# High parts of output-projection inputs on VectorE inside attention, two first sums on ScalarE, and the turns of the rotary tables two products behind their copies

## The chip, the cores and the metric

The kernel runs on one core of one Trainium2 chip. Times are device microseconds (us) of one execution of the whole program; of several runs the median is given. A core has TensorE (PE, matrix products), VectorE (DVE), ScalarE (ACT), GpSimd (POOL) and SyncE (SP, which here only starts DMAs). Matrix products land in PSUM; everything else works out of SBUF. Each engine takes its own instructions strictly in the order in which the program lists them, and waits on semaphores for the others.

## The reference

One decoder block, 2048 positions, 1024 channels, f32 throughout. The input projection makes eight column groups; one group goes through a short convolution and a gated linear recurrence, three through attention in three dilated windows with partial rotary positions, the rest are gates.

```python
proj = h @ w_in[l]
x_rnn, z_rnn, q, k, v, z_attn, g_r, g_a = jnp.split(proj, IN_SPLITS, axis=-1)
hr = rg_lru(causal_depthwise_conv(x_rnn, ...), w_a, b_a, w_x, b_x, lam, positions)
y_rnn = (hr * jax.nn.silu(z_rnn)) @ w_out_rnn[l]
qh, kh = apply_partial_rope(q, cos, sin), apply_partial_rope(k, cos, sin)
o = dilated_attention_mixture(qh, kh, vh).reshape(B, S, D_ATTN)
y_attn = (o * jax.nn.silu(z_attn)) @ w_out_attn[l]
merged = jax.nn.sigmoid(g_r + bg_r) * y_rnn + jax.nn.sigmoid(g_a + bg_a) * y_attn
x = x + gate[:, None, :] * (merged @ w_o[l])
return rms_norm(x, g_final)
```

Rotary positions need `cos` and `sin` of position times frequency. The change touches how a table of these is brought into the layout of q and k, how sums of products are taken out of PSUM in the input projection, and how the inputs of `y_rnn` and `y_attn` are made ready for TensorE.

## The kernel before

**Split operands.** TensorE multiplies in a rounded f32 format (`fp32r`). To keep f32 accuracy each operand is split into a high part, a copy that rounds (`hi_act` on ScalarE, L162, or `hi_dve` on VectorE, L165), and a low part, the rest that the subtraction leaves (`lo_pool` on GpSimd, L168, or `lo_dve` on VectorE, L171). A product is three matmuls, high by high, high by low, low by high (`mm3`, all at L154). These helpers stand behind nearly every row of a view: rows are told apart by their tiles, not by their lines.

**Input projection.** It runs in two halves of the positions, `f` = 0 and 1, as Strassen-like pairs of column blocks: `strassen` makes seven products for each pair, each of 12 matmuls, into the PSUM tiles X, Z, W, V, Y. The order on TensorE is X (`B11`), the V (`B22`) that the pair before has left over, Z, W, V (`T1`), X (`B21`), Y. Four sums are needed; the first is a copy of X to SBUF, `u1`, to which Z is added for `u2`. The left operands S are made from raw loads R by GpSimd, VectorE and ScalarE in the first half, stored to DRAM (`sD`) by DMAs on ScalarE's queue, and in the second half reloaded from there for the first 20 pairs. All side work is hung on the count of products: `after_prod[n]` and `late[n]` hold functions that are called after product n, and the scheduler of the framework then keeps each engine's order near to that.

**Recurrence and tables.** Between the pairs the recurrence of each block of channels runs on VectorE and ScalarE. The rotary tables are made in each half, four pieces each (two column halves q, and i = 0 for cosine, 1 for sine), which begin at products 90, 94, 111 and 116 behind the half's start (`PIECES`). A piece has three steps: `repeat` (L1087, VectorE copies a 128x64 block of the table, repeated four times, into a 128x512 tile), `turn` (L1092, four 128x128 transposes on TensorE into the PSUM tile `pg`), and `store` (L1098, ScalarE copies `pg` to SBUF for the cosine; L1100, VectorE multiplies it by a sign for the sine; then L1101, a DMA on SP's queue to the table `tabD`). In the first half the tiles of `repeat` and `store` come from a ring of three buffers `ev`, from which the gates' tiles (L460, stored to `zaT` at L1255) are taken as well; in the second half they are raw tiles R, the ring of five into which weights are loaded as well.

**Attention with the output projection inside.** From about 1345 to 1880 us the 16 head-halves (8 heads, two halves of the queries) run as a sequence of slots under `manual_schedule`, which keeps the program order exactly. Each slot has five places: HEAD, the scores of one tile and their softmax (L1489 on VectorE, L1490 on ScalarE), SOFTMAX, EXCHANGE, WEIGHTS, then the transposes of the probabilities of the tile seven slots earlier (`pT` at L1575 and L1588, split into `pth` and `ptl`) and the products with the values (`sc`, `o`), TAIL. Between these places `spend` fills TensorE with steps of the output projection: job j is one block of 512 positions of `yaT` (j = 0 to 3, the recurrence's branch) or `oT` (j = 4 to 7, the attention's), with 8 output tiles m of 8 steps k, three matmuls each, into the PSUM tile `pj`. Jobs 0 to 3 and most of job 4 run inside attention, job 5 to 7 behind it.

**Inputs of a job.** A job's input is eight 128x512 tiles (k = 0 to 7). `load_y` loads one into a buffer R0 to R3; `split_y` splits it into `yh` and `yl` (rings of nine). Two tables of step numbers, relative to the job's start, say when each load and each split is listed:

```python
    LOAD_Y = {-12: [0], -10: [1], -8: [2], -6: [3], -2: [4], 4: [5], 5: [6], 6: [7]}
    SPLIT_Y = {-3: [0], 3: [1], 4: [2], 5: [3], 7: [4], 10: [5], 11: [6], 12: [7]}
```

So a split's high and low part stand in the engines' order wherever the step lands between the places of a slot. GpSimd makes the low part of even k and VectorE that of odd k; GpSimd splits the heads' `kq`, `vh` and `wh` beside it.

Of the kernel before, what the change touches and what calls it, by code (L numbers as in the profile page):

```python
# [14 lines left out]
AF = mybir.ActivationFunctionType  # L15
# [9 lines left out]
NB = 4  # L25
# [10 lines left out]
MORE = 0.8  # L36
FIRST = 4.0
REBUILT = 20
COPIED = (5, 22)
NEG = 1e30  # L40

TABLES = 24
# [50 lines left out]
def decoder_block(ctx, tc, x, c, positions, g_norm, w_mod, b_mod, w_in, b_gate, conv_w, conv_b,  # L93
                  w_a, b_a, w_x, b_x, lam, w_out_rnn, w_out_attn, w_o, g_final, cst, out):
    nc = tc.nc
# [65 lines left out]
    def hi_act(o, i):  # L161
        nc.scalar.activation(o, i, AF.Copy)  # L162
# [152 lines left out]
    def load_next():  # L315
        n = n_loaded[0]
        n_loaded[0] += 1
        if n < REBUILT * 7:
            t = s_tile([P, 2, KH, P])
            nc.sync.dma_start(t[:].bitcast(F32), sD[n])  # L320
            loaded.append((n, t))
        elif n >= 28 * 7:
            k = n - 28 * 7
            for y in range(2 * k - 2, 2 * k) if k in (1, 2) else ():
                load_yd(yaT, 0, y)
            if k < 3:
                load_wd(0, 0, k) if k < 2 else load_wd(0, 1, 0)
            if k == 1:

                t = T(hp, [P, KH, CH], F32, "T", bufs=14)  # L330
                nc.sync.dma_start(t[:], yaT[KH * P :, :CH].rearrange("(k p) j -> p k j", p=P))
                for i in range(KH):
                    Y0[True, 0, KH + i] = t[:, i, :]
# [17 lines left out]
    def strassen(f, key, done):  # L351

        up = pu[0]
        x = pair_id[key]
        if f and x == 0:
            for _ in range(NS):
                load_next()
        n_op = iter(range(7 * x, 7 * x + 7))

        def take():  # L360
            if f and x < REBUILT:
                return (f, *loaded.pop(0))
            i = next(n_op)
            return f, i, first.pop(i)

        def prod(ps, b, first, last, op=None):
            f, i, s = op or take()
            bh, bl = B[b]
            for k in range(KH):
                mm3(ps[:], s[:, 0, k, :], s[:, 1, k, :], bh[:, k, :], bl[:, k, :],  # L370
                    first=first and k == 0, last=last and k == KH - 1, skip_group_check=True)
            n_prod[0] += 1
            if f:
                used.add(i)
                while n_loaded[0] - NS in used:
                    load_next()
            run_late(n_prod[0])

        X = T(pj, [P, CH], F32, "X", bufs=2)
        prod(X, "B11", True, False)  # L380
        last_product()
        Z = T(pj, [P, CH], F32, "Z")
        prod(Z, "T2", True, True)
        u1 = T(up, [P, CH], F32, "u1", bufs=1)
        u2 = T(up, [P, CH], F32, "u2", bufs=2)
        with tc.high_priority():
            if not f and x in COPIED:
                nc.vector.tensor_copy(u1[:], X[:])
            else:
                nc.scalar.activation(u1[:], X[:], AF.Copy)  # L390
            nc.vector.tensor_tensor(u2[:], Z[:], u1[:], ALU.add)
        W = T(pj, [P, CH], F32, "W")
        prod(W, "T3", True, True)
        u3 = T(up, [P, CH], F32, "u3", bufs=1)
        with tc.high_priority():
            nc.vector.tensor_tensor(u3[:], W[:], u2[:], ALU.add)
        V = T(pj, [P, CH], F32, "V")
        prod(V, "T1", True, False)
        done(1, 1, V, u3)
        prod(X, "B21", False, True)  # L400
        done(0, 0, X, None)
        Y = T(pj, [P, CH], F32, "Y")
        prod(Y, "T4", True, True)
        done(1, 0, Y, u3)
        op = take()

        def last():
            prod(V, "B22", False, True, op)
            done(0, 1, V, u2)
        behind.append(last)  # L410
# [4 lines left out]
    def last_product():  # L415
        while behind:
            behind.pop()()
# [622 lines left out]
    def rotary_tables(rp, f):  # L1040

        v = {}

        def angles():
            pi = T(rp, [P, 2, 4], I32, "pi")
            nc.sync.dma_start(pi[:], positions[0].rearrange("(n j r) -> j n r", n=NB, r=4)[:, 2 * f : 2 * f + 2, :])
            v["pi"] = pi
            for tag in ("an", "kk", "co"):
                v[tag] = T(rp, [P, 8, 16], F32, tag)

        def convert():
            v["pf"] = T(rp, [P, 8], F32, "pf")
            nc.vector.tensor_copy(v["pf"][:], v["pi"][:].rearrange("p n r -> p (n r)"))

        def products():
            nc.vector.tensor_tensor(
                v["an"][:], v["pf"][:].unsqueeze(2).broadcast_to([P, 8, 16]),
                cs[:, K_IF : K_IF + 128].rearrange("p (b f) -> p b f", f=16), ALU.mult)

        flat = lambda tag: v[tag][:].rearrange("p b f -> p (b f)")  # L1060
        magic = 1.5 * 2.0 ** 23
        tensor = lambda dst, src, s1, s2, *ops: lambda: nc.vector.tensor_scalar(flat(dst), flat(src), s1, s2, *ops)

        def reduce(per, bits, n):
            yield tensor("kk", "an", float(1 / per), None, ALU.mult)
            yield tensor("kk", "kk", magic, None, ALU.add)
            yield tensor("kk", "kk", -magic, None, ALU.add)
            for cc in split_const(per, bits, n):
                yield lambda cc=cc: nc.vector.scalar_tensor_tensor(flat("an"), flat("kk"), -cc, flat("an"), ALU.mult, ALU.add)

        def shifted():
            nc.vector.scalar_tensor_tensor(flat("co"), flat("an"), math.pi / 2, flat("kk"), ALU.add, ALU.add)

        lim = 3.1415925
        quarter = (tensor("kk", "an", math.pi / 2, -float(TWO_PI), ALU.is_gt, ALU.mult), shifted,
                   *(tensor(tag, tag, lim, -lim, ALU.min, ALU.max) for tag in ("an", "co")))

        def sines():
            for tag in ("an", "co"):
                nc.scalar.activation(flat(tag), flat(tag), AF.Sin)  # L1080

        def piece(q, i):

            def repeat():
                src = v[("co", "an")[i]]
                v["rep"] = raw_tile([P, 4, 8, 16]) if f else T(rp, [P, 4, 8, 16], F32, "ev", bufs=3)
                nc.vector.tensor_copy(v["rep"][:], src[:, 4 * q : 4 * q + 4, :].unsqueeze(2).broadcast_to([P, 4, 8, 16]))  # L1087

            def turn():
                v["pt"] = T(pg, [P, 4, P], F32, "pg")  # L1090
                for r in range(4):
                    nc.tensor.transpose(v["pt"][:, r, :], v["rep"][:, r].rearrange("p a b -> p (a b)"), ident)  # L1092

            def store():
                t = raw_tile([P, CH]) if f else T(rp, [P, CH], F32, "ev", bufs=3)
                pt = v["pt"][:].rearrange("p r j -> p (r j)")
                if i == 0:
                    nc.scalar.activation(t[:], pt, AF.Copy)  # L1098
                else:
                    nc.vector.tensor_scalar(t[:], pt, cs[:, K_SG : K_SG + 1], None, ALU.mult)  # L1100
                nc.sync.dma_start(tabD[f, i, :, q * CH : (q + 1) * CH], t[:])  # L1101

            return repeat, turn, store

        at_, base = TABLES, n_prod[0]
        for fn in (angles, None, convert, products, *reduce(TWO_PI * 4096, 7, 8), *reduce(TWO_PI, 11, 5), *quarter, None, sines):
            if fn:
                after_prod.setdefault(base + at_, []).append(fn)
            at_ += 1
        assert at_ <= PIECES[0]  # L1110

        for x, (q, i) in enumerate((q, i) for q in range(2) for i in range(2)):
            for d, fn in zip((0, 3, 4), piece(q, i)):
                after_prod.setdefault(base + PIECES[x] + d, []).append(fn)

    def load_tables(qp, f):
# [59 lines left out]
    for t in range(6):  # L1176
        pieces = []
        i0 = t * P
        while i0 < (t + 1) * P:
            hd, i = divmod(i0, 96)  # L1180
# [547 lines left out]
    def steps(jobs):  # L1728
# [39 lines left out]
        def split_y(j, k):  # L1768
            if j < len(jobs):
                Y[j, k] = yh, yl = [T(fl, [P, CH], F32R, tag, bufs=NY) for tag in ("yh", "yl")]  # L1770
                w, ys, n = jobs[j]
                t = Y0.pop((ys is yaT, n, k))
                hi_act(yh[:], t[:])
                (lo_dve if (k % 2 if j else k > 4) or j > NB + 1 else lo_pool)(yl[:], t[:], yh[:])

        def load_g(t):
# [27 lines left out]
        for t, (j, m) in enumerate(tiles):  # L1804
            ps = T(pj, [P, CH], F32, "pj")
            for k in range(KT):
                x = 2 * t + k // KH
# [25 lines left out]
                yh, yl = Y[j, k]  # L1833
# [5 lines left out]
                x = m * KT + k - KT * (KT - 1)  # L1839
                j1 = j + 1  # L1840
                if m == 0:
                    x, j1 = x + KT * KT, j
# [309 lines left out]
    with tc.manual_schedule():  # L2152
# [10 lines left out]
        for p in range(NP):  # L2163
            for d, fn, args in left_events(p):
                x = 7 * p + d - 4
# [54 lines left out]
```

## Time and profile before

| | us |
|---|---|
| median of three runs | 2177.58 |
| the three runs | 2177.54, 2182.49, 2177.58 |
| the profiled execution, as timed | 2177.2 |
| its span, first to last instruction | 2175.4 |
| granted clock of TensorE, mean | 0.999 |
| DMA, mean over the span | 240 GB/s |

The profile is of one further execution. Its page gives the busy time of each engine and the chain of waits that ends last. A view of waits gives, for each engine, what an instruction waited for: engine, tile, line, then the sum in us, the number of waits and the longest. In a timeline a row is start, length, engine, line, operation, written tile, then "<-" and the tiles read, and in square brackets the idle time of the engine before it with whoever ended it. `sc`, `pT`, `pj`, `pg`, X, Y, Z, W and V are PSUM tiles; the others lie in SBUF or, for `zaT`, `yaT`, `tabD`, `sD`, in DRAM. A row of one tile's instructions gives least, median and greatest duration in ns, and the first and last start.

### The profile page before, as it was taken

How to read it: one execution, taken by the hardware profiler on the slowest of the kernel's cores; microseconds unless marked ns; L12 is line 12 of the kernel's file. 1: busy time of each engine (PE TensorE's matmuls, PEld its weight loads, DVE VectorE, ACT ScalarE, POOL GpSimd, SP SyncE). 2: the span in 40 equal slices, each digit the busy share in tenths (PEclk: the TensorE clock that was granted, in tenths of full speed). 3: DMA queues.
4: the chain of work that ended last, by engine and by line, in shares of the span. 5: the costliest groups of instructions: out<-in, count | busy, mean ns of one | idle time of the engine just before them, and what ended most of it. 6: DMA issues, size and time to landing. Idle time of an engine off the chain costs nothing.

```text
span 2175.4 us, 32659 instructions
## 1 busy us (share of the span) xinstructions
PE 2144.5 (99%) x10570; PEld 1788.8 (82%) x10571; DVE 1482.4 (68%) x2570; ACT 1311.0 (60%) x2621; POOL 1110.7 (51%) x868
## 2 busy tenths in 40 slices
PE   9999999999999999999999999999999999999998
PEld 6888788788788888888888887888888988888886
DVE  6769877768656715545546675577767777688887
ACT  5748678568644527457457532688888887444333
POOL 1467677667666323223223575466666674422444
PEclk9999999999999999999999999999999999999999
DMA  8467887787655368898996566988886777898552
GB/s 302 142 213 262 275 300 268 270 285 244 176 116 164 107 230 289 297 307 307 321 327 238 160 165 182 286 270 265 264 269 213 254 235 231 301 320 296 181 172 109
DMA packets 413040, 522.98 MB, mean 240 GB/s; under 512 B 103142, under 2 KB 278466, under 8 KB 411844
## 3 DMA queue, kind: packets, MB, share of 16 engines
q1 hardware_dynamic: 372852, 403.22, 59.2%
q10 hardware_dynamic: 34384, 99.78, 12.3%
q0 software_dynamic: 5632, 17.88, 2.4%
q8 instruction: 84, 1.38, 0.3%
q14 instruction: 88, 0.72, 0.1%
HBM read 332.02 MB, written 188.75 MB: 239 GB/s over the span
## 4 chain that ended last, share of the span: by engine, by line
PE 57%; DMA 4%; DVE 4%; ACT 3%; issue 3%; POOL 2%; SPq 0%; POOLq 0%; ACTq 0%; DVEq 0%
PE X L154 11%; PE V L154 11%; PE pj L154 8%; PE Z L154 6%; PE W L154 6%; PE Y L154 5%; PE sc L154 3%; PE o L154 3%; DMA fg<-gaT 1%; PE pg L154 1%; DMA fg<-mrT 1%; ACT pp L1490 1%; PE pT L1575 1%; DMA vraw<-vN 1%; PE pT L1588 1%
## 5 line engine op out<-in xcount | busy, mean ns | idle before, releaser
L168 POOL TENSOR_TENSOR S<-R,S 128x512 fp32r<-128x512 f32 x192 | 296.0, 1549 | 176.8 <-ACT S L162 85.5
L154 PE MATMUL X<-T,S 128*128 128x512 f32 x1344 | 324.2, 390 | 3.4 <-ACT u L390 1.6
L154 PE MATMUL V<-T,S 128*128 128x512 f32 x1344 | 324.8, 390 | 0.5 <-DVE ev L460 0.2
L154 PE MATMUL pj<-yh,S 128*128 128x512 f32 x896 | 324.2, 403 | 0.0
L154 PEld LDWEIGHTS X<-T,S 128*128 128x128 f32 x1344 | 251.4, 188 | 58.8 <-ACT u L390 3.6
L154 PEld LDWEIGHTS V<-T,S 128*128 128x128 f32 x1344 | 251.4, 188 | 55.6 <-DVE xr L460 1.1
L168 POOL TENSOR_TENSOR S<-s,S 128x512 fp32r<-128x512 f32 x116 | 170.6, 1471 | 149.3 <-ACT S L162 106.4
L154 PEld LDWEIGHTS pj<-yh,S 128*128 128x128 f32 x896 | 168.2, 188 | 30.1 <-DVE S L171 1.1
L154 PE MATMUL pj<-yl,S 128*128 128x512 f32 x448 | 175.8, 392 | 0.4 <-POOL yl L168 0.2
L162 ACT ACTIVATE S<-s 128x512 fp32r<-128x512 f32 x124 | 77.4, 624 | 150.6 <-DVE s L287 104.9
L1490 ACT ACTIVATE pp<-pp,st 128x256 f32<-128x256 f32 (+3 forms) x256 | 133.5, 523 | 54.8 <-DVE st L1489 53.9
L154 PE MATMUL W<-T,S 128*128 128x512 f32 x672 | 162.1, 390 | 0.0
L154 PE MATMUL Y<-T,S 128*128 128x512 f32 x672 | 161.5, 389 | 0.0
L154 PE MATMUL Z<-T,S 128*128 128x512 f32 x672 | 161.4, 389 | 0.0
L162 ACT ACTIVATE S<-R 128x512 fp32r<-128x512 f32 x200 | 121.5, 623 | 59.4 <-issue 15.2
L171 DVE TENSOR_TENSOR ptl<-pT,pth 128x384 fp32r<-128x384 f32 (+1 forms) x160 | 97.9, 629 | 81.7 <-ACT pth L162 79.5
L154 PEld LDWEIGHTS W<-T,S 128*128 128x128 f32 x672 | 125.7, 188 | 26.8 <-issue 0.9
L154 PEld LDWEIGHTS Z<-T,S 128*128 128x128 f32 x672 | 126.1, 188 | 26.2
L154 PEld LDWEIGHTS Y<-T,S 128*128 128x128 f32 x672 | 126.1, 188 | 26.1
L168 POOL TENSOR_TENSOR s<-R,s 128x512 fp32r<-128x512 f32 x32 | 44.3, 1386 | 186.4 <-ACT s L162 166.6
L979 DVE SCALAR_TENSOR_TENSOR xc<-xr,par,xc 128x512 f32<-128x512 f32 x96 | 103.2, 1075 | 53.2 <-ACT xc L973 50.9
L1555 ACT ACTIVATE pp<-pp,M 128x256 f32<-128x256 f32 (+3 forms) x256 | 118.1, 523 | 7.5 <-DVE M L1678 7.3
(424 smaller groups left out, 4939.6 us busy)
## 6 DMA issues: line engine op xcount, KB each, us to landing
sD<-S ACTq DMA_DIRECT2D x140, 512.0 KB, 3.6
S<-sD SPq DMA_DIRECT2D x140, 512.0 KB, 5.2
S<-wD SPq DMA_DIRECT2D x82, 512.0 KB, 5.4
R<-in_w_in_dram SPq DMA_DIRECT2D x144, 256.0 KB, 3.3
wD<-s ACTq DMA_DIRECT2D x64, 256.0 KB, 4.7
kraw<-kqT SPq DMA_DIRECT2D x32, 384.0 KB, 5.1
T<-in_w_mod_dram SPq DMA_DIRECT2D x16, 512.0 KB, 8.9
vN<-ev SPq DMA_DIRECT2D x32, 256.0 KB, 2.6
```

What stands on the lines that cost most here:

```text
L154: nc.tensor.matmul(o, lhsT=l, rhs=r, start=st, stop=sp, **kw)
L162: nc.scalar.activation(o, i, AF.Copy)
L168: nc.gpsimd.tensor_tensor(o, i, h.bitcast(F32), ALU.subtract)
L171: return nc.vector.tensor_tensor(o, i, h.bitcast(F32), ALU.subtract).ins
L979: nc.vector.scalar_tensor_tensor(xc, xr[:, i : i + CH], cw(i), xc, ALU.mult, ALU.add)
L1490: nc.scalar.activation(pdst, pdst, AF.Exp, bias=m_, scale=-1.0, accum_out=l_)
L1555: nc.scalar.activation(pp, pp, AF.Copy, scale=w)
L1575: nc.tensor.transpose(pt[:, c0 + j * P : c0 + (j + 1) * P], pp[i][:, k * P : (k + 1) * P], ident)
L1588: nc.tensor.transpose(pt[:, c * P : (c + 1) * P], pp[:, half * P : (half + 1) * P], ident)
```

## The change

It has three parts. In `split_y`, the high part of the jobs 1 to 4, 32 copies, is made by VectorE (`hi_dve`) where ScalarE made it; the low parts stay. In `strassen`, the constant that named the pairs 5 and 22 goes, whose `u1` in the first half was copied by VectorE; ScalarE copies it as for all other pairs. In `rotary_tables`, `turn` is called two products after `repeat` in place of three, and `store` three in place of four.

```diff
-COPIED = (5, 22)
...
         with tc.high_priority():
-            if not f and x in COPIED:
-                nc.vector.tensor_copy(u1[:], X[:])
-            else:
-                nc.scalar.activation(u1[:], X[:], AF.Copy)
+            nc.scalar.activation(u1[:], X[:], AF.Copy)
             nc.vector.tensor_tensor(u2[:], Z[:], u1[:], ALU.add)
...
         for x, (q, i) in enumerate((q, i) for q in range(2) for i in range(2)):
-            for d, fn in zip((0, 3, 4), piece(q, i)):
+            for d, fn in zip((0, 2, 3), piece(q, i)):
                 after_prod.setdefault(base + PIECES[x] + d, []).append(fn)
...
                 t = Y0.pop((ys is yaT, n, k))
-                hi_act(yh[:], t[:])
+                (hi_dve if 0 < j < NB + 1 else hi_act)(yh[:], t[:])
                 (lo_dve if (k % 2 if j else k > 4) or j > NB + 1 else lo_pool)(yl[:], t[:], yh[:])
```

Since lines go, the numbers behind them are lower by one (the helpers) or by four (what follows `strassen`) in the program after the change. A row of the lists below is line, operation, written tile, "<-", tiles read, shape; numbers in names count tiles.

**VectorE, attention, at 1624 us of the profile.** The softmax of one tile of scores (L1489), then the low part of an odd input tile (`yl_16039`), then the splits of transposed probabilities (`pth`, `ptl`). Before:

```order
L1489 ISA pp_16015,st_15697<-sc_16011,msk_12088 128x512
L1489 ISA st_15697 128x1
L171 TENSOR_TENSOR yl_16039<-R_2999_15733,yh_16038 128x512
L165 CAST pth_16047<-pT_16042 128x512
L171 TENSOR_TENSOR ptl_16048<-pT_16042,pth_16047 128x512
L165 CAST pth_16056<-pT_16051 128x512
L171 TENSOR_TENSOR ptl_16057<-pT_16051,pth_16056 128x512
```

After:

```order
L1485 ISA pp_16015,st_15697<-sc_16011,msk_12088 128x512
L1485 ISA st_15697 128x1
L164 CAST yh_16027<-R_2984_15663 128x512
L164 CAST yh_16038<-R_2999_15733 128x512
L170 TENSOR_TENSOR yl_16039<-R_2999_15733,yh_16038 128x512
L164 CAST pth_16047<-pT_16042 128x512
L170 TENSOR_TENSOR ptl_16048<-pT_16042,pth_16047 128x512
L164 CAST pth_16056<-pT_16051 128x512
L170 TENSOR_TENSOR ptl_16057<-pT_16051,pth_16056 128x512
```

Two casts of `yh` have come in ahead of the low part and of all the splits behind it; the first (`yh_16027`, an even tile) is for a low part on GpSimd.

**ScalarE, first half, at the first piece of the tables, near 390 to 405 us.** `sg` are the gates' sigmoids, `S` operand splits, `u` the copy of X, `htail` the recurrence's carry, `ev` the table's store. Before:

```order
L1244 ACTIVATE sg_3743<-ev_3726 128x512
L162 ACTIVATE S_692_3750<-s_663_3594 128x512
L281 DMA sD<-S_681_3676 128x1024
L390 ACTIVATE u_694_3756<-X_3684 128x512
L1020 ACTIVATE htail_601<-y_3616 128x1
L1098 ACTIVATE ev_3781<-pg_3745 128x512
```

After:

```order
L1240 ACTIVATE sg_3748<-ev_3731 128x512
L1094 ACTIVATE ev_3750<-pg_3721 128x512
L161 ACTIVATE S_693_3753<-s_663_3594 128x512
L280 DMA sD<-S_681_3676 128x1024
L386 ACTIVATE u_695_3759<-X_3684 128x512
L1016 ACTIVATE htail_601<-y_3616 128x1
```

The table's copy (L1098, now L1094) has moved from behind the operand split, `u` and `htail` to ahead of them.

**TensorE, first half, at the second piece, near 401 to 408 us.** Before, X is followed by all of Y (12 matmuls) and then by the four transposes of the turn; the last row of Y, the turn, and the first of the next X:

```order
L154 MATMUL Y_3846<-T_903,S_687_3722 128x512
L154 MATMUL Y_3846<-T_902,S_687_3722 128x512
L1092 MATMUL pg_3867<-cs_60,ev_3784 128x128 x4
L154 MATMUL X_3881<-T_138,S_702_3790 128x512
L154 MATMUL X_3881<-T_139,S_702_3790 128x512
```

After:

```order
L153 MATMUL X_3684<-T_141,S_686_3702 128x512
L153 MATMUL X_3684<-T_140,S_686_3702 128x512
L1088 MATMUL pg_3833<-cs_60,ev_3784 128x128 x4
L153 MATMUL Y_3851<-T_902,S_688_3727 128x512
L153 MATMUL Y_3851<-T_903,S_688_3727 128x512
```

The turn now stands ahead of Y, between the last matmul of X and Y's first; on SP's queue the first piece's store to `tabD` has moved ahead of a load of R and of a store to `yaT` in the same way.

## Prediction

> **What bounds the kernel.** I read the page first (busy times, then the chain), then the waits of each engine in the attention stage, then the timeline around each place that the change touches.
>
> ```profile
> span 2175.4 us, 32659 instructions
> PE 2144.5 (99%) x10570; PEld 1788.8 (82%) x10571; DVE 1482.4 (68%) x2570; ACT 1311.0 (60%) x2621; POOL 1110.7 (51%) x868
> PE 57%; DMA 4%; DVE 4%; ACT 3%; issue 3%; POOL 2%; SPq 0%; POOLq 0%; ACTq 0%; DVEq 0%
> ```
>
> TensorE is busy for 2144.5 of 2175.4 us, so it bounds the kernel, and everything that other engines do counts only where it makes TensorE wait. There are 30.9 us of such idle time in all. No matmul is added or removed, so a gain has that ceiling; a loss has none. The high parts move inside attention, so that stage is read by itself (row: stretch, length, then busy time and count of PE, weight loads, DVE, ACT, POOL).
>
> ```profile
> 1400.00:1600.00 200.00, 198.46 (x1300) 175.64 (x1300) 145.85 (x450) 162.56 (x501) 128.71 (x125) 1.00 0.86 269
> 1600.00:1880.00 280.00, 271.60 (x1781) 243.49 (x1780) 201.88 (x511) 225.08 (x557) 167.58 (x131) 1.00 0.76 240
> PE sc L154 <- DVE st L1489: 3.9, 4, 2.4
> PE pT L1575 <- DVE ptl L171: 2.4, 3, 1.3
> PE pT L1575 <- ACT pp L1555: 2.0, 5, 0.9
> PE sc L154 <- POOL q L1451: 0.8, 2, 0.4
> PE pj L154 <- POOL yl L168: 0.2, 1, 0.2
> ```
>
> Over these 480 us ScalarE is busy 387.6 us (81%), VectorE 347.7 (72%), GpSimd 296.3 (62%). TensorE waits 9.3 us: 6.3 end with VectorE, 2.0 with ScalarE, 1.0 with GpSimd. The engine that is relieved is the busiest beside TensorE, but the engine that gets its work ends three times as much of TensorE's waiting.
>
> **Part 1: 32 high parts from ScalarE to VectorE.** What goes and what stays:
>
> ```profile
> L162 ACT ACTIVATE yh<-R x32: 614/618/632, 1402.6 to 1778.4; 128x512 fp32r<-128x512 f32 x32
> L168 POOL TENSOR_TENSOR yl<-R,yh x16: 1283/1294/1734, 1404.9 to 1775.1; 128x512 fp32r<-128x512 f32 x16
> L171 DVE TENSOR_TENSOR yl<-R,yh x16: 677/693/1975, 1414.5 to 1779.1; 128x512 fp32r<-128x512 f32 x16
> DVE yl L171 <- ACT yh L162: 17.1, 9, 3.5
> ```
>
> ScalarE is rid of 32 x 0.618 = 19.8 us. VectorE's own low parts (the odd tiles) waited 17.1 us for ScalarE's high part in 9 of 16 cases; that handoff is gone. The price of a copy on VectorE has two ends:
>
> ```profile
> L1451 DVE CAST q<-kq x4: 418/421/422, 1364.3 to 1368.1; 128x512 fp32r<-128x512 f32 x4
> 388.19 1.73 POOL L168 TENSOR_TENSOR S<-R,S 128x512 fp32r<-128x512 f32 x1
> 388.70 1.51 DVE L1087 COPY ev<-co 128x512 f32<-128x512 f32 x1
> ```
>
> The same cast costs 0.42 us alone. A copy of this size issued at 388.70, while GpSimd worked until 389.92, took 1.51 us and ended 0.29 us after GpSimd did. So the bounds are 0.42 and 1.51 us. GpSimd is busy 62% of this stage with pieces of about 1.3 us; a copy that comes at a random moment meets one with that chance, waits half of it and needs 0.29 us more: 0.38 x 0.42 + 0.62 x (0.65 + 0.29) = 0.74 us, an estimate. 32 of them are 24 us. VectorE goes to 347.7 + 24 = 372 us, ScalarE to 387.6 - 19.8 = 368: even. [...]
>
> Whether 24 us fit into idle time is read at the places. The dearest of VectorE's waits:
>
> ```profile
> 1624.60 1.57 POOL L168 TENSOR_TENSOR wh<-vraw,wh 128x640 fp32r<-128x640 f32 x1 [5.32 <-ACT wh L162]
> 1626.12 3.68 POOL L168 TENSOR_TENSOR kq<-kraw,kq 128x768 fp32r<-128x768 f32 x2
> 1628.37 1.98 DVE L171 TENSOR_TENSOR yl<-R,yh 128x512 fp32r<-128x512 f32 x1 [3.50 <-ACT yh L162]
> 1630.27 0.68 DVE L165 CAST pth<-pT 128x512 fp32r<-128x512 f32 x1
> ```
>
> VectorE idles 3.5 us here for two high parts, and TensorE then waits for the pth and ptl behind. With the change two copies stand at 1624.86 instead. The first ends 0.29 us after GpSimd's wh, at 1626.46; the second meets the first kq (to 1627.96) and ends near 1628.2; the low part meets the second kq and, as before, ends half a microsecond behind it, at 1630.3. The pth starts when it started before: the idle time is spent, nothing is gained. The next stall behind it:
>
> ```profile
> 1640.73 1.88 POOL L168 TENSOR_TENSOR kq<-kraw,kq 128x768 fp32r<-128x768 f32 x1
> 1642.29 0.86 DVE L171 TENSOR_TENSOR yl<-R,yh 128x512 fp32r<-128x512 f32 x1 [1.40 <-ACT yh L162]
> 1643.08 0.34 DVE L1655 TENSOR_TENSOR xq<-sc,cs 128x64 f32<-128x64 f32 x2
> 1647.44 0.30 PE L1575 MATMUL pT<-cs,pp 128*128 128x128 f32 x1 [0.86 <-ACT pp L1555]
> ```
>
> The copy now starts at 1640.8, ends behind kq at 1642.9, and the low part at 1643.6 or later instead of 1643.15. Queued behind it on VectorE are xq, the maxima and the weights M; ScalarE scales the probabilities by M and TensorE transposes them, already 0.86 us late. I take +0.8 us for it. On GpSimd a piece hit by a VectorE one takes 1.73 instead of 1.29 us (the rows at 388.19 and of the yl): +0.4 us at each of the two waits for q, +0.9 in all. Against it, ScalarE has no yh between the softmax and the gather and pth: half of the 2.0 us of waits for pp and of the 0.2 us for yl (-1.1) and 0.5 us of the wait for st. That is +0.1. About a dozen copies stand where VectorE had no idle time, at 0.42 us and more each, 5 us; TensorE has projection matmuls in line between the heads' pieces, so I let half, 2.5 us, through. Part 1: **+2.6 us**, between -6 (two thirds of the 9.3 us go) and +9 (half of 24 us less the idle 17.1 x 0.35 reach TensorE).
>
> **Part 2: two first sums copied by ScalarE.** At pair 5:
>
> ```profile
> 238.19 0.61 ACT L162 ACTIVATE S<-s 128x512 fp32r<-128x512 f32 x1
> 238.86 0.68 DVE L388 COPY u<-X 128x512 f32<-128x512 f32 x1
> 239.69 2.97 PE L154 MATMUL X<-T,S 128*128 128x512 f32 x12 [1.34 <-DVE u L388]
> L390 ACT ACTIVATE u<-X x54: 575/580/601, 130.2 to 1332.6; 128x512 f32<-128x512 f32 x54
> ```
>
> TensorE waits 1.34 us for VectorE's copy, which ends at 239.54. ScalarE's copy stands behind the S<-s: 238.72 + 0.58 = 239.3. Gain 0.24, between -0.3 (ScalarE late by a piece) and 1.3. At pair 22 the copy is at 580.9 and X is needed four products later: nothing, and 0.6 us on ScalarE hidden behind the same four. Part 2: **-0.2 us**.
>
> **Part 3: the turns one product earlier.** A turn reads the repeated rows that VectorE copies (L1087), so it may now wait for them:
>
> ```profile
> 397.66 0.69 DVE L460 TENSOR_TENSOR ev<-V,u 128x512 f32<-128x512 f32 x1 [1.21 <-DMA zaT<-ev]
> 401.41 3.02 PE L154 MATMUL X<-T,S 128*128 128x512 f32 x12
> 404.27 2.88 PE L154 MATMUL Y<-T,S 128*128 128x512 f32 x12
> 407.47 0.43 DVE L1087 COPY ev<-an 128x512 f32<-128x512 f32 x1 [2.71 <-DMA zaT<-ev]
> 407.95 0.66 PE L1092 MATMUL pg<-cs,ev 128*128 128x128 f32 x4 [0.80 <-DVE ev L1087]
> ```
>
> If the copy stayed at 407.47, the turn, now ahead of Y at 404.2, would wait 3.7 us instead of 0.8. But the earlier store also passes a buffer of the ring on: the gate's ev at 397.66 no longer waits for a store (1.2 us earlier), and the copy waits for the first table's store, issued near 399.8, not for the gate's. It can start when VectorE reaches it, 404.1, and end at 404.5; the turn waits 0.4 us. Gain 0.4. The same two products on, at the fourth piece:
>
> ```profile
> 463.73 0.58 ACT L390 ACTIVATE u<-X 128x512 f32<-128x512 f32 x1
> 464.36 3.01 PE L154 MATMUL X<-T,S 128*128 128x512 f32 x12
> 469.62 0.68 DVE L396 TENSOR_TENSOR u<-W,u 128x512 f32<-128x512 f32 x1
> 469.93 2.88 PE L154 MATMUL X<-T,S 128*128 128x512 f32 x12
> 471.56 0.46 DVE L1087 COPY ev<-an 128x512 f32<-128x512 f32 x1 [1.26 <-DMA tabD<-ev]
> ```
>
> The store's copy (0.58 us) now stands ahead of u on ScalarE, u ends at 464.9 and X starts 0.5 us late. The turn moves from 472.65 to 470.4, and the copy, with the table's store gone out earlier, follows L396 at 470.3 and ends at 470.7: 0.3 us more. Loss 0.8, of which the wait for V behind the old turn gives 0.3 back. On SP's queue the table's store now stands ahead of a weight load (2 us later, needed four products on) and in the second half ahead of reloads that were issued seven products early. Pieces 1, 3 and the second half have 4 to 10 us between copy and turn. Part 3: **+0.1 us**, between -0.8 and +5.
>
> **Sum.** +2.6 - 0.2 + 0.1 = +2.5 us on a span of 2175.4, whose run took 2177.2; the median of the runs is 2177.58, 0.4 above. On the median: **2180.1 us**, +0.11%.
>
> **Rivals.** [...] Copies wait for GpSimd's pieces, not for chance moments: GpSimd works in rows of pieces when ScalarE has just fed it, and the copies stand there. For it: 1.51 against 0.42 us, and the place at 1628 where nothing is gained. Against it: 17.1 us of idle VectorE to spend. At 1.1 us each, 35 us less the 17 idle leave 18; it decides once half of that reaches TensorE: 2177.6 + 9 = 2186.6. *Faster.* ScalarE, at 81%, was the late one; the handoffs go, and VectorE's lateness with them. Two thirds of 9.3 us, the 1.3 of pair 5 and 0.8 of the turn: 2177.6 - 8.3 = 2169.3. [...] *The turns don't come earlier.* If the copies still wait for their stores, TensorE loses 2.9 us at 404 and 2.1 at 470: 2177.6 + 5 + 1.3 = 2183.9.
>
> **How the numbers follow.** Forecast 0.42; slower by the port 0.40; faster 0.12; the turns' waits 0.06. About 0.3% (6.5 us: 2171.1 to 2184.1) is what a measurement of this kernel can tell from no change. The forecast and the turns lie inside: 0.48 within, 0.40 slower, 0.12 faster. The forecast's own range is 2172 to 2184; that for 8 in 10 takes in most of both rivals: 2170 to 2190.
>
> **What would show it.** VectorE's casts of yh near 0.74 us on average (0.42: the port doesn't matter here; above 1: the port rival); TensorE's waits from 1400 to 1880 at 10 to 14 us, still ended mostly by VectorE; VectorE and ScalarE near 77% there; the wait at 407.95 under 0.8 us and the fourth piece's under 0.5; X of pair 5 still waiting about 1 us, now for ScalarE. The forecast is wrong if TensorE's waits there halve, or pass 16 us.

## The result, and the profile after

| | before | changed |
|---|---|---|
| median, us | 2178.84 (22 runs) | 2175.14 (22 runs) |
| least and greatest, us | 2176.01, 2183.84 | 2172.04, 2180.72 |
| profiled execution: span, granted clock | 2175.4, 0.999 | 2175.5, 0.997 |

The ratio is 0.9982, 95% interval 0.9975 to 0.9990: the change makes the kernel faster by 0.18%, some 4 us. The forecast was slower by 2.5 us. The time lies inside the range of 2170 to 2190; the direction was wrong.

The two profiled executions have the same span, so the gain is not to be read off there: in the changed one TensorE was granted a clock of 0.83 from 1355 to 1365 us and of 0.86 and 0.80 from 1642 to 1647 and from 1647 to 1652, where the kernel before shows 1.00 (1355 to 1365 and 1640 to 1650). The page of the changed kernel:

```profile
span 2175.5 us, 32647 instructions
PE 2144.2 (99%) x10570; PEld 1792.5 (82%) x10571; DVE 1503.7 (69%) x2600; ACT 1296.3 (60%) x2591; POOL 1112.1 (51%) x868
```

Attention, first by windows (stretch, length, busy time and count of PE, weight loads, DVE, ACT, POOL, then clock), and the group of the casts (count, busy time, mean ns):

```profile
1400.00:1600.00 200.00, 199.08 (x1315) 177.77 (x1315) 155.67 (x468) 156.38 (x493) 131.15 (x125) 1.00 0.86 270
1600.00:1880.00 280.00, 270.10 (x1760) 242.01 (x1759) 215.11 (x525) 214.66 (x532) 166.10 (x130) 0.99 0.76 237
...
L164 DVE CAST yh<-R 128x512 fp32r<-128x512 f32 x32 | 23.3, 734 | 0.0
```

Then TensorE's waits from 1400 to 1880 us (sum, times, longest):

```profile
PE sc L153 <- DVE st L1485: 5.4, 4, 2.2
PE pT L1571 <- ACT pp L1551: 2.7, 6, 1.4
PE pT L1571 <- DVE ptl L170: 1.3, 2, 0.7
PE sc L153 <- POOL q L1447: 0.6, 2, 0.5
PE pj L153 <- POOL yl L167: 0.3, 1, 0.3
```

VectorE is busy 370.8 us there (forecast 372), ScalarE 371.0 (368), a cast takes 0.734 us (0.74), TensorE waits 10.3 us (10 to 14). Part 1 does what was worked out, and in this stage there is no gain. It must lie elsewhere. The rows of the second and the fourth table piece, VectorE's copy and TensorE's turn:

```profile
404.56 0.42 DVE L1083 COPY ev<-an 128x512 f32<-128x512 f32 x1
405.03 0.66 PE L1088 MATMUL pg<-cs,ev 128*128 128x128 f32 x4 [0.56 <-DVE ev L1083]
...
463.28 2.88 PE L153 MATMUL X<-T,S 128*128 128x512 f32 x12
467.70 0.42 DVE L1083 COPY ev<-an 128x512 f32<-128x512 f32 x1
468.72 0.60 PE L1088 MATMUL pg<-cs,ev 128*128 128x128 f32 x4
```

The copies wait for nothing any more (2.71 and 1.26 us before), the turn at 405 still for 0.56 us, and the X of the fourth piece, which the forecast had 0.5 us late, isn't.

### The profile page after: what moved, and what is told of

It reads as the page before. It is cut to its first block, busy times and chain, and to the rows that moved or that the text cites. A ratio compares the mean times of both kernels' runs of the same rounds, so it can differ in the third digit from the quotient of the medians.

```text
span 2175.5 us, 32647 instructions
## 1 busy us (share of the span) xinstructions
PE 2144.2 (99%) x10570; PEld 1792.5 (82%) x10571; DVE 1503.7 (69%) x2600; ACT 1296.3 (60%) x2591; POOL 1112.1 (51%) x868
## 4 chain that ended last, share of the span: by engine, by line
PE 61%; DVE 6%; DMA 3%; ACT 2%; issue 1%; POOL 1%; SPq 0%; POOLq 0%; DVEq 0%; ACTq 0%
PE X L153 11%; PE pj L153 11%; PE V L153 11%; PE Z L153 6%; PE W L153 6%; PE Y L153 5%; PE sc L153 4%; PE o L153 4%; PE pT L1571 1%; PE pg L153 1%; PE pT L1584 1%; DVE ptl L170 1%; DVE pp L1485 1%; DVE yh L164 1%; ACT pp L1486 1%
```

## The experiments

Where the time goes was followed by the place of the same product: its start in one profile less its start in another. The table is worked out from TensorE's timelines against a second profile of the kernel before (b2, below); negative is earlier, and a column changes where time is won or lost. The rows are stations in b2's time. Two profiles are left out for width: p2 stands 1.3 to 1.6 us behind b2 from 400 us on, and p1k at -0.8, -2.7, -1.6 and -1.0 at the last four stations. Each column is one execution: the first shows how far two profiles of the same kernel differ, 0.4 us here; behind one place near 400 us it can be 1 to 2 us (below).

```
us     before    p3  after   s33   t24  p3f0 p3f0b    p1   p1o   p1e    fx   fxk   fxo
 390    -0.60 -0.56  -0.03 -0.16 -0.02 -0.03 -0.31 -0.84  0.44 -0.15 -0.30 -0.61 -0.82
 415    -0.29 -1.17  -0.53 -0.50  1.68  0.55 -0.97 -0.60  2.56  0.27 -0.85 -1.15 -1.34
 430    -0.25 -1.89  -1.25 -1.22  0.96 -0.17 -1.69 -0.58  2.59  0.27 -1.57 -1.87 -2.06
 490    -0.16 -3.09  -2.44 -1.34  0.34 -1.36 -2.89 -0.50  2.89  0.48 -2.76 -3.06 -3.26
 600    -0.25 -3.99  -3.03 -1.88 -0.88 -2.19 -3.59 -0.55  2.83  0.43 -3.70 -4.00 -4.23
1340    -0.22 -3.97  -3.03 -1.85 -0.88 -2.16 -3.57 -0.31  2.85  0.44 -3.67 -3.98 -4.22
1368    -0.41 -1.01  -0.90 -2.94 -1.61  1.00 -4.39 -0.90  2.99  2.11 -3.34 -2.51 -4.60
1600    -0.40 -1.24  -2.81 -3.14 -1.88  0.71 -4.68 -2.77  0.95  1.24 -5.27 -4.42 -6.70
1700    -0.37 -1.20  -1.73 -3.02 -1.89  0.73 -4.59 -3.23 -0.68 -1.10 -5.72 -4.86 -8.37
1870    -0.34 -1.17   0.33 -3.01 -1.87  0.73 -4.53 -1.20 -0.48 -1.25 -3.72 -4.20 -7.77
```

The ratios, all to the kernel before on the same chip, from 10 to 12 runs of each kernel:

| run | what | median, us | ratio and interval |
|---|---|---|---|
| p1 | part 1 alone | 2179.14 | 1.0002 (0.9993 to 1.0011) |
| p2 | part 2 alone | 2177.84 | 0.9994 (0.9985 to 1.0002) |
| p3 | part 3 alone | 2173.62 | 0.9978 (0.9970 to 0.9987) |
| b2 | before again | 2180.14 | 1.0007 (0.9998 to 1.0016) |
| s33 | store at three, turn at three | 2177.46 | 0.9994 (0.9986 to 1.0003) |
| t24 | turn at two, store at four | 2177.83 | 0.9992 (0.9984 to 1.0001) |
| p3f0, p3f0b | part 3, first half only, twice | 2176.40, 2174.74 | 0.9991 (0.9981 to 1.0000), 0.9982 (0.9973 to 0.9991) |
| fx | changed, extra steps ahead of the first scores | 2174.50 | 0.9977 (0.9968 to 0.9986) |
| fxk | fx, one cast back on ScalarE | 2173.48 | 0.9980 (0.9971 to 0.9988) |
| p1k | p1, the same cast back | 2177.81 | 1.0000 (0.9991 to 1.0009) |
| fxo | fx, casts of odd k only | 2172.01 | 0.9972 (0.9963 to 0.9981) |
| p1o | part 1, odd k only | 2177.39 | 0.9994 (0.9985 to 1.0003) |
| p1e | part 1, even k only | 2175.71 | 0.9991 (0.9982 to 0.9999) |

**The parts one by one.** Each is the kernel before with the lines of one part.

> Part 3 alone. Theory A (the gain comes from the turns: TensorE's small waits between 395 and 550 us go, 3.0 us in the profile before against 0.9 after): 0.9982 to 0.9990 of the time before, and DVE no longer waits 2.7 us for zaT at the second table piece. Theory B (the gain comes from attention, where the profile after has spells of a lower granted clock that hide it): 0.9995 to 1.0005.

> Part 1 alone: the 32 high parts on VectorE. Theory A: no gain in attention, 0.9995 to 1.0012, TensorE's waits from 1400 to 1880 us 9 to 12 us as in both profiles. Theory B: 0.9980 to 0.9988, the waits there at 6 us or less where the clock is full.

> Part 2 alone: u1 of pairs 5 and 22 on ScalarE. Both theories: within 0.5 us of before (0.9997 to 1.0002), X of pair 5 waiting 1.0 us for ScalarE in place of 1.3 for VectorE, nothing at pair 22.

> The kernel before, once more, for a second profile and the clock of each run: 0.9993 to 1.0007. It shows how far TensorE's small waits differ between two profiles of one kernel. Theory A: its waits between 395 and 550 us are 3.0 us within 0.5 again. Theory B: they are as often 1 us.

Part 3 alone gives 0.9978, part 1 1.0002, part 2 0.9994, the kernel before 1.0007: theory A. The gain is the turns'. In us they are -4.8, +0.4 and -1.3, together more than the -3.9 of the whole, but the intervals are some 2 us wide to either side. In the table p3 and the changed kernel win 3.4 and 3.0 us between 390 and 600 us, and nothing in the second half (600 to 1340). The same in the windows view, as products done in one stretch, b2 first:

```profile
395.00:550.00 155.00, 153.53 (x674) 123.89 (x673) 117.93 (x122) 105.38 (x174) 108.25 (x72) 1.00 0.74 257
```

and p3:

```profile
395.00:550.00 155.00, 154.55 (x687) 127.44 (x686) 123.47 (x125) 106.20 (x175) 110.06 (x73) 1.00 0.76 259
```

13 matmuls more in the same 155 us, at 0.23 us apart (the 12 of Y at 404.27 us in the kernel before take 2.88 us, one alone 0.39), are 3.0 us. TensorE's idle time shows only a third of that, 1.5 us in b2 against 0.45 in p3. The 3.0 us that the expectations of p3 and b2 took for the waits before are not there; both profiles of the kernel before have 1.5. The wait of the turn is only 0.3 us of the gain (0.75 in b2, 0.45 in p3). Most of the rest, 2.2 us, is won at three places behind, where the recurrence multiplies its input by gates: 0.7 us each at 420, 482 and 544 us; 0.5 us more come near the fourth piece. The last of them in b2, TensorE's first two matmuls and GpSimd's low part `xl` of their input:

```profile
543.86 0.39 PE L154 MATMUL pg<-xh,gh 128*128 128x512 f32 x1
544.54 0.50 PE L154 MATMUL pg<-xl,gh 128*128 128x512 f32 x1 [0.29 <-POOL xl L168]
...
542.75 1.73 POOL L168 TENSOR_TENSOR xl<-xc,xh 128x512 fp32r<-128x512 f32 x1
```

In p3:

```profile
540.77 0.39 PE L154 MATMUL pg<-xh,gh 128*128 128x512 f32 x1
541.00 0.39 PE L154 MATMUL pg<-xl,gh 128*128 128x512 f32 x1
...
538.79 1.74 POOL L168 TENSOR_TENSOR xl<-xc,xh 128x512 fp32r<-128x512 f32 x1
```

`xl` ends at 544.48 in b2, 0.4 us after TensorE could take it, and at 540.53 in p3, 0.5 us before. The lateness comes down a chain: VectorE makes the recurrence's input, ScalarE its high part, GpSimd its low part. VectorE is 3.8 us earlier in p3 behind the second piece, 1.0 us of it from ahead of the copy, where the gate's `ev` waits in b2, and 2.7 since the copy no longer waits. TensorE is only 1.2 us earlier; the difference is cover. Every profile with the old turns at three and four (before, b2, p1, p2) has the waits at these places, none with part 3 has them.

**Which step of part 3.**

```diff
-            for d, fn in zip((0, 3, 4), piece(q, i)):
+            for d, fn in zip((0, 3, 3), piece(q, i)):
```

This is s33, the store moved and the turn not; t24 has `(0, 2, 4)` there, the turn moved and the store not.

> The table's store three products behind the copy in place of four, the turn left at three. Theory C (what pays is the earlier store: it frees the buffer for which VectorE's copy waited 2.7 us at the second piece and 1.3 us at the fourth, and VectorE's lateness no longer reaches the recurrence's products at 419, 481 and 543 us): as part 3 alone, 0.9970 to 0.9985, VectorE's waits there gone. Theory D (what pays is the turn's own place, one product ahead): 0.9993 to 1.0007.

> The turn two products behind the copy, the store left at four. Theory C: the copy of the second piece still waits 2.7 us for zaT, and the turn, now ahead of Y, waits for it: 3 to 4 us in place of 0.8, no gain: 1.0000 to 1.0020. Theory D: 0.9970 to 0.9985.

Neither alone brings the gain. In s33 VectorE's copy doesn't wait, as theory C has it, but TensorE waits for `u`:

```profile
405.54 0.41 DVE L1087 COPY ev<-an 128x512 f32<-128x512 f32 x1
...
402.27 3.02 PE L154 MATMUL X<-T,S 128*128 128x512 f32 x12 [0.43 <-ACT u L390]
464.20 3.06 PE L154 MATMUL X<-T,S 128*128 128x512 f32 x12 [0.73 <-ACT u L390]
...
462.55 0.60 ACT L1098 ACTIVATE ev<-pg 128x512 f32<-128x512 f32 x1 [1.33 <-DMA kqT<-ev]
```

At both places the store's copy now stands ahead of `u` on ScalarE, which is what was forecast for the fourth piece. It does so in p3 as well, but there ScalarE comes early enough: near 464 us `u` starts 3.1 us earlier than in b2, X 1.9, and `u` ends 1.3 us before X starts. In s33 the gate's `ev` still waits 1.15 us for its store ahead of the first place, and the table's copy itself 1.33 us for a buffer ahead of the second (the last row). s33 wins 1.7 us in the table where p3 wins 3.4; these two waits are 1.2 us of the difference. In t24 the copy waits as before and the turn waits for it:

```profile
407.25 0.66 PE L1092 MATMUL pg<-cs,ev 128*128 128x128 f32 x4 [2.77 <-DVE ev L1087]
...
406.77 0.43 DVE L1087 COPY ev<-an 128x512 f32<-128x512 f32 x1 [2.72 <-DMA zaT<-ev]
```

The forecast had just this as a rival (2.9 us here, and 2.1 at the fourth piece, where the turn waits only 0.35). But the kernel is not slower: 0.9992. By 600 us TensorE stands 0.9 us ahead of b2 all the same, since the waits at 420, 482 and 544 are gone here too: a TensorE that comes 2 us later doesn't find VectorE late (in p2 and p1o, where VectorE is late with it, the waits are there). So theories C and D both fail in part: the 3 us are TensorE's share of VectorE's lateness, and it is paid once, wherever it shows.

**First half only.**

```diff
+            for d, fn in zip((0, 3, 4) if f else (0, 2, 3), piece(q, i)):
```

> Part 3 in the first half alone; the second half's turns as before. Theory C: the whole gain, 0.9970 to 0.9987, since the second half has another ring and TensorE waits nowhere in it in either profile. Rival: half of it belongs to the second half (SP's queue, reloads), 0.9985 to 0.9995.

> Part 3 in the first half alone, once more. In its first profile TensorE stood where part 3 alone puts it everywhere but near 401 and 405 us, where ScalarE was 1.8 us later, though the two programs list the same instructions up to 690 us. If that was one execution's chance: 0.9975 to 0.9988, and a place at 550 us within 0.5 us of that of part 3 alone. If the second half matters: 0.9988 to 0.9996 again, with TensorE's place at 550 us as in part 3 alone.

The first time 0.9991, in the rival's range, with 2.2 us won between 390 and 600; the second time 0.9982, in that of chance, with 3.3 (at 550 us 0.3 us from p3). The two intervals overlap. In the first, ScalarE was 1.7 us late near 398 us and X waited for `u`; p2 and p1o, whose programs are those of before at this place, show V waiting 1.35 and 1.86 us there. One execution differs from the next by 1 to 2 us at this one place. The second half of part 3 shows no effect in the traces (nothing won between 600 and 1340 us with or without it).

**What is given back where attention begins.** p3 and the changed kernel lose 3.0 and 2.1 us of it between 1340 and 1368. The changed kernel there, the scores waiting for `kq`, two matmuls behind them, and the window with its clock:

```profile
1357.25 0.33 PE L153 MATMUL sc<-kq 128*128 128x128 f32 x1 [2.19 <-ACT kq L161]
...
1359.32 1.05 PE L153 MATMUL pj<-yh,S 128*128 128x512 f32 x2
...
1355.00:1365.00 10.00, 7.41 (x28) 5.95 (x28) 4.51 (x11) 4.79 (x9) 1.27 (x1) 0.83 0.92 343
```

TensorE waits longer for `kq` than before (2.19 against 1.47 us), and then its matmuls stand 0.43 us apart for some 3 us at a clock of 0.83 (two took 0.62 us in all before, here 1.05). That it waits longer because it comes earlier is not shown. The loads of `kq` are issued earlier too (1349.64 us here, 1352.17 in b2), and the wait doesn't follow TensorE's place: s33, 1.9 us ahead of b2, waits 0.5 us, p3f0b, 3.6 us ahead, 0.8, and p1o, 2.9 us behind, 1.8.

```diff
-            owed += rate + (MORE if 0 <= s <= NU else 0.0) + (FIRST if s == 0 else 0.0)
+            owed += rate + (MORE if 0 <= s <= NU else 0.0) + (FIRST if s == -1 else 0.0)
```

> The changed kernel with the four extra projection steps of the first slot of attention placed one slot earlier, ahead of the first scores. Theory E (part of the gain is given back where attention begins: TensorE arrives 2.7 us earlier, waits 2.2 us for kq in place of 1.5, and its matmuls then take 0.63 us in place of 0.39 for 3 us): the wait is under 0.5 us, the slow matmuls are gone, 0.9965 to 0.9976. Rival (the wait only moves to the second scores near 1365 us): 0.9978 to 0.9986.

```profile
1358.33 0.50 PE L153 MATMUL pj<-yh,S 128*128 128x512 f32 x1 [2.55 <-DVE fg L1785]
...
1359.84 0.85 PE L153 MATMUL sc<-kq 128*128 128x128 f32 x6
...
1356.98 0.69 DVE L170 TENSOR_TENSOR kq<-kraw,kq 128x512 fp32r<-128x512 f32 x1 [0.62 <-ACT kq L161]
1357.59 0.68 DVE L1785 TENSOR_TENSOR fg<-pj,fg 128x512 f32<-128x512 f32 x1
```

The scores no longer wait for `kq`, but the next projection tile now waits 2.55 us for an eviction (`fg`). That stands on VectorE behind the low parts of `kq`, and these wait for the same loads; the eviction's gate had landed at 1353.2 us. So the wait moved, if not where the rival had it, and no slow matmuls followed it (clock 1.00 from 1350 to 1365 us). In the table fx loses 0.3 us here in place of 2.1; the run, 0.9977, can't be told from the changed kernel's 0.9982. p3f0b had no loss here (a wait of 0.8 us), so this too differs from one execution to the next, and what is given back here can't be put down to the change.

**Why part 1 gives nothing.** In the table p1, the changed kernel and fx win 1.9 us each between 1368 and 1600, and lose 2.0 between 1700 and 1870. fx at the place, VectorE's rows and TensorE's wait:

```profile
1766.59 1.48 DVE L164 CAST yh<-R 128x512 fp32r<-128x512 f32 x1
1768.10 2.23 DVE L170 TENSOR_TENSOR yl<-R,yh 128x512 fp32r<-128x512 f32 x1
1770.25 1.14 DVE L170 TENSOR_TENSOR ptl<-pT,pth 128x512 fp32r<-128x512 f32 x2
...
1772.95 0.46 PE L153 MATMUL sc<-sm,msk 128*128 128x128 f32 x2 [2.17 <-DVE st L1485]
```

The cast and the low part take 1.48 and 2.23 us beside GpSimd's `vh` (1766.47 to 1767.78) and `kq` (1767.73 to 1769.78), and the softmax behind them is late. With GpSimd idle the kernel before has 0.42 us for a cast of this size (`q`, from 1364.3 us on) and 0.69 for a low part (`kq`, at 1363.71).

```diff
-                (hi_dve if 0 < j < NB + 1 else hi_act)(yh[:], t[:])
+                (hi_dve if 0 < j < NB + 1 and (j, k) != (4, 5) else hi_act)(yh[:], t[:])
```

This is fxk against fx and p1k against p1. In fxo and p1o the condition is `and k % 2` in its place, in p1e `and not k % 2`.

> The changed kernel, the four extra steps ahead of the first scores, and one of the 32 high parts (job 4, k = 5) back on ScalarE. Theory F (part 1 gains 2 us before 1700 and gives them back at this one place: the cast waits behind GpSimd's vh, the low part behind it behind kq, the softmax is late and TensorE waits 2.2 us for st near 1770, its matmuls then at 0.63 us for 3 us): that wait under 0.5 us, 2.5 to 4 us less than without the edit: 0.9955 to 0.9970. Rival (another of the 32 takes its place, or ScalarE is late instead): 0.9972 to 0.9982.

> Part 1 alone without that one high part. Theory F: 0.9980 to 0.9993 where all 32 gave 1.0002. Rival: 0.9997 to 1.0007.

A miss. The wait fell from 2.17 to 0.81 us, now for ScalarE, as the rival had it, and behind 1760 us both profiles lose 1.3 us less (0.7 in place of 2.0), half of what theory F forecast; in the runs, 0.9980 and 1.0000, nothing of it can be seen.

> The changed kernel with the extra steps ahead of the first scores, and only the 16 high parts of odd k on VectorE, whose low parts VectorE makes too. If the gain of part 1 is the handoff that goes and its price the casts behind GpSimd's pieces, half the price is left and all of VectorE's part of the gain: 0.9965 to 0.9978; the wait near 1770 stays, since k = 5 is among them. If relief of ScalarE is the gain, 0.9980 to 0.9988.

> Part 1 for odd k alone (16 casts), the rest as before. Theory G (the odd casts gain, since VectorE no longer waits for ScalarE ahead of its own low part, and the even ones, which VectorE makes for GpSimd, give it back): 0.9978 to 0.9992, TensorE's waits from 1400 to 1880 us 6 to 7.5 us. Theory H (gain and price lie in both alike): 0.9994 to 1.0006, 9 to 10 us.

> Part 1 for even k alone (16 casts), the rest as before. Theory G: 1.0005 to 1.0022, TensorE's waits from 1400 to 1880 us 11 us or more. Theory H: 0.9994 to 1.0006, 9 to 10 us.

Half the casts, odd or even, is better than all of them in the profiles. TensorE's busy time and matmuls done between 1400 and 1880, for p1o:

```profile
1400.00:1880.00 480.00, 473.13 (x3104) 424.05 (x3103) 364.10 (x983) 382.97 (x1053) 298.74 (x255) 1.00 0.81 254
```

for p1e:

```profile
1400.00:1880.00 480.00, 472.37 (x3103) 422.54 (x3102) 359.74 (x979) 383.41 (x1050) 297.66 (x256) 1.00 0.81 253
```

and for all 32, p1:

```profile
1400.00:1880.00 480.00, 470.53 (x3080) 421.01 (x3080) 372.15 (x993) 372.43 (x1025) 298.73 (x256) 1.00 0.80 252
```

Either half wins 3.4 us between 1368 and 1870 (2.99 to -0.48, 2.11 to -1.25), fxo 3.2, and all 32 win 0.3 in p1. TensorE is idle for 6.9 (odd) and 7.6 us (even) there, against 9.5 with all 32. So neither G nor H: both halves gain alike in the profiles, and it is the sum of the two that costs. A cast doesn't become dearer by it (0.83 us each in p1o, 0.81 in p1e, 0.74 in p1), but VectorE's low parts do. The group of these 16 in the kernel before, in p1 and in p1e (count, busy time, mean ns):

```profile
L171 DVE TENSOR_TENSOR yl<-R,yh 128x512 fp32r<-128x512 f32 x16 | 14.3, 893 | 17.1 <-ACT yh L162 17.1
...
L171 DVE TENSOR_TENSOR yl<-R,yh 128x512 fp32r<-128x512 f32 x16 | 18.6, 1162 | 0.6
...
L171 DVE TENSOR_TENSOR yl<-R,yh 128x512 fp32r<-128x512 f32 x16 | 14.3, 892 | 11.7 <-ACT yh L162 11.7
```

With all 32 casts they take 4.3 us more in all, with the odd ones 2.3, with the even ones nothing. VectorE's load in the stage grows from 347 to 364 (odd), 360 (even) and 372 us (all). Whether the low parts or the last 10 us of load make the sum too dear was not tried by itself, and the cause stays open. The wait near 1770 us, which was expected to stay in fxo, is 0.65 us there though the same cast is on VectorE, so the casts around it count as well. In the runs p1o and p1e are 0.9994 and 0.9991, with intervals that overlap p1's. fxo is the fastest version that was run, 0.9972, as expected (0.9965 to 0.9978); its interval overlaps fx's (0.9977) and the changed kernel's (0.9982).

## Why the prediction was wrong

**The step that failed** is part 3's term: "+0.1 us, between -0.8 and +5". The mechanism it named was right: the earlier store passes a buffer on, the copy starts when VectorE reaches it (404.1 forecast, 404.56 seen), the turn waits 0.4 us (0.56 seen). The size was not. The forecast took the turn's 0.80 us for all that VectorE's 2.71 us cost TensorE, and so "Gain 0.4" and a lower end of -0.8. The experiments put it at 3.0 to 3.4 us in the traces (2.2 in the first of p3f0), and at 0.9978 (0.9970 to 0.9987) for the kernel, 4.8 us (2.8 to 6.5). Of what was missing 2.2 us stood in three places 15 to 140 us behind, where matmuls start 0.1 to 0.45 us later than 0.23 us apart; most of these gaps are too short for the view of waits. That VectorE's lateness reaches TensorE there, through ScalarE's and GpSimd's parts of the recurrence's input, was not in the forecast.

**The fourth piece** was priced at a loss of 0.8, with `u` late. It didn't come with part 3, but did with the store alone moved (s33: 0.73 us). The order on ScalarE was forecast rightly; what was left out is that ScalarE comes earlier along with VectorE: `u` starts 3.1 us earlier there in p3, X only 1.9.

**Part 1**, +2.6 us with -6 to +9, measured 1.0002 (0.9993 to 1.0011), that is +0.4 us (-1.5 to +2.4): no loss that can be told from nothing, and too dear by some 2 us. At 1624 the forecast sequence came nearly as written (the pair of casts 2.68 us, the low part 2.22; `pth` starts at 1627.24, 3.0 us before its old time, of which 2.4 us had been won ahead of it, so 0.6 us were gained where the forecast had nothing). The slower rival, +9, needed 1.1 us a copy; at 0.73 us each, the estimate for chance moments, it is out. The port after which the chances name it is shown by no run: the runs show casts of 0.41 to 2.07 us in the changed kernel, their median 0.42 and their mean 0.734. The low parts that became dearer (0.89 to 1.16 us each) and the place at 1766 were not foreseen. That VectorE's load came out (370.8 us for 372) is partly luck: the low parts' 4.3 us were not in the sum, and its other work was some 4 us less.

**Part 2**, -0.2: 0.9994 (0.9985 to 1.0002), not to be told from nothing; X of pair 5 waits for ScalarE as forecast:

```profile
240.19 3.04 PE L153 MATMUL X<-T,S 128*128 128x512 f32 x12 [1.00 <-ACT u L386]
```

**The rivals.** "Faster" had the right direction for the wrong reason: it counted on attention, where TensorE's waits went from 9.3 to 10.3 us; a cast took 0.73 us on VectorE there, where ScalarE had needed 0.62. "The turns don't come earlier" was tried as t24; its 2.8 us wait came, its loss didn't. Its 2183.9 adds 1.3 us without saying from what; with the +2.4 of parts 1 and 2 it would be 2185.0.

The forecast's own test, TensorE's waits in attention, came out inside its bounds (10.3 us). It said nothing on the first half beyond the turns' own waits.

## What to carry to other kernels

A stall on an engine that isn't the bottleneck is priced by what it leaves late, not by the one instruction that is seen waiting for it: follow the chain that starts there to the next places where the bottleneck meets it, and compare the starts of the same work in two traces, since waits too short for a table add up. A wait moved to the bottleneck isn't a loss if the bottleneck would have met the same lateness later. And a load moved from one engine to another is better tried in halves: here either half won 3.4 us in its stage in the profiles and the whole almost nothing, though the runs can't tell the three apart.

## What the hardware showed beyond that

After waits of 2.19 us (changed kernel) and 3.01 us (p3) at 1357 us, 128x512 matmuls started 0.43 us apart in place of 0.23, for some 3 us. In p1e TensorE was idle for 2.06 us between 1355 and 1365 us (busy 7.94 us of the 10), and the clock there was 0.85; with a wait of 2.55 us in fx (1358 us, clock 1.00) it wasn't lowered. A wait of 2.42 us for `st` that ended at 1640.43 us in the kernel before was followed by none of this (clock 1.00 from 1640 to 1645); in p3f0b, 4 us ahead there, the clock was 0.73 from 1635 to 1640, with TensorE busy for 3.85 us of the 5. So a wait of 2 to 3 us has a slow stretch behind it in some of these profiles and not in others; what decides it is not shown.
